# A hybrid mLSTM and RWKV-7 encoder layer: the mixer's TensorE steps taken in the written order

## The chip, the core and the metric

The kernel runs on one core of a Trainium2 chip. The metric is the device time of one execution in microseconds (us); it is the median of several executions. The core has a matrix engine (TensorE, PE in the rows), a vector engine (VectorE, DVE), an activation engine (ScalarE, ACT), GpSimd (POOL) and SyncE (SP, which issues most transfers). Each engine works through its own queue of instructions in order, and waits where an instruction needs a result that another engine has not yet delivered.

## What is computed

One encoder layer for 2048 tokens of width 1024. Only the mixer matters here, and the preparation of the attention behind it:

```python
h = rmsnorm(x, norm_mix);  p = h @ w_in
# first half of the columns: mLSTM, 4 heads of 128, chunks of 64
q, k = silu(causal_dwconv(p_qk));  gates = p_gates + m_gate_b
logf = log_sigmoid(f_pre);  b = cumsum(logf)            # per chunk
p    = exp(b_t - b_s + logi_s - m_t) * (q @ k.T)        # causal
h    = (s_int * (c_prev @ q) + p @ v) / max(|den|, exp(-m_t))
# second half: RWKV-7, 8 heads of 64, one state per head
sk    = state @ kk
state = state * w - outer(sk, kk * a) + outer(v, k);  y = state @ r
y_r   = (groupnorm(y) + sum(r * k * r_rk) * v) * sigmoid(gd) @ r_g_up
x = x + concat(y_m, y_r) @ w_out
kv = rmsnorm(mem) @ w_kv      # 256 memory rows, for the cross attention
```

Behind it come the cross attention to mem, a gated feed-forward network with a short convolution, and a last norm. All inputs and outputs are float32.

## The kernel before

**Tiling.** `mixer()` takes the tokens in 4 blocks of TB = 512. Each block needs 31 column groups of the projection (first x14, which holds the inputs of the gates, then x12 and the r, k, v and q, k, v, o groups), each as 24 dense matmuls of 128 by 512: the weights and the activations are split into a high and a low part, and three of the four products are computed for 8 slices of the depth. The rest of the mixer comes in units of one mLSTM head, or two RWKV heads, over one block; there are 16 units of each kind.

**Streams.** The work is written as generators, each of which yields after a small piece. `st_dense` (projection, `proj`, tile pd), `st_gates` (the gates of a block, `gates`, L486), `st_ml` (an mLSTM unit, `mlstm`, L833), `st_pre` (an RWKV unit's inputs and the small matrices of its chunks, last tile pab), `st_merge` (merges the solved matrices), `st_seq` (`rwkv_seq`, L730: the chain of 8 steps over the chunks of a unit) and `st_tail` (`rwkv_tail`, L774: group norm, transposes py, gate pg). `run_streams` (L1071) goes through them by a reckoned clock and writes next the first stream in the order s, g, a, t, m, p, d that is ready by that clock. A stream says with `yield` how long its next piece will have to wait for other engines; these waits are numbers of nanoseconds at L279 to L282, for instance LE and LME ahead of the mLSTM's pn and LSOLVE ahead of a merge. LG, the wait ahead of the gates' transposes, is 0:

```python
        LF, LG, LGD, LQK, LFD, LME, LM1 = 1590, 0, 1147, 3611, 844, 676, 3063
        ...
        order = dict(a=st_gates, s=st_seq, t=st_tail, m=st_ml, g=st_merge, p=st_pre, d=st_dense)
        run_streams([order[c]() for c in "sgatmpd"])
        kv_prep(kt, sm, T, PQ, PD)
```

**What sets the order.** The order in which the streams are written is not the order in the engines' queues. A scheduler takes the written instructions and puts those of each engine in an order of its own, by its own reckoning of what is ready when. That holds for all five engines and for the whole mixer.

**Names.** Nearly all matmuls of the mixer go through `mm` and `tr`, so their lines are L122 and L126; the tiles tell them apart. Gates: pd (of x14), then the chain L488 to L522 on ScalarE and VectorE over 4 rows, then four transposes gtr and their copy gc (L533). mLSTM unit: transposes pvt and pkt, products pst (k with q), e (L858 to L866, ScalarE and VectorE), then four times pn and pc, at the end the transposes pht. RWKV unit: pab; pt, p and pe belong to the solve and the merge. Each step of `rwkv_seq`: products into qy, ScalarE's copy q (L747), pu, VectorE's copy UV (L755), pS, VectorE's new state sbd (L761), further products into qy, ScalarE's copy yt.

**kv_prep** (L171) is called at the end of `mixer()`. For the norm of mem it needs two small matmuls mbc; then it handles 4 heads, each with eight weight loads of 512 KB (two of w_k, two of w_qT, two of w_v, two of w_ov) and the matmuls kps, qkps, kps again and vops, 672 in all. A weight load (`load_w`, L112) takes one of two raw buffers and is split by ScalarE (high) and GpSimd or VectorE (low).

Of the kernel before, what the change touches and what calls it, by code (L numbers as in the profile page):

```python
# [56 lines left out]
def tile_hybrid_encoder(ctx: ExitStack, tc: tile.TileContext, t_in: dict, out: bass.AP, stage: str = "all"):  # L57
# [1055 lines left out]
        kv_prep(kt, sm, T, PQ, PD)  # L1113
        mx.close()

    mixer()
    wld[0] = 0
    if stage == "mix":
        nc.sync.dma_start(out, y_dram.rearrange("k p t -> (k p) t"))
# [361 lines left out]
```

## Time and profile before

| | us |
|---|---|
| median of 3 runs | 3570.65 (3564.45 to 3571.49) |
| the profiled execution: its own time | 3564.44 |
| its span in the trace | 3562.6 |
| TensorE busy, of the span | 3377.6 (95%) |
| VectorE busy | 2020.6 (57%) |
| ScalarE busy | 1256.2 (35%) |
| GpSimd busy | 1368.7 (38%) |

The span is the time from the first to the last record of the profiled execution. The mixer takes the first 1431 us of it, the rest of kv_prep lasts until about 1514, and the attention and the feed-forward network the rest. Busy shares of the whole span hide that VectorE is far busier in the mixer than behind it; the table of stretches below has that. In the rows, a float32 matmul through L122 is recorded twice, so x8 in the trace is x4 in the order; transposes are recorded once, and so are the dense matmuls.

### The profile page before, as it was taken

What the parts mean: (1) busy time and instruction counts of PE and PEld (TensorE: products, weight loads), DVE (VectorE), ACT (ScalarE), POOL (GpSimd) and SP (SyncE); (2) the same over time, 40 slices, a digit from 0 to 9 for tenths busy, and PEclk for the clock granted to TensorE, in tenths of its full rate; (3) what the DMA queues carried; (4) which work ended last, traced back from release to release, by engine and by line L of the source; (5) the groups of instructions that cost most, each with busy time, mean ns of one, the idle gap of its engine ahead of it and who ended that gap; (6) DMA issues with size and microseconds to landing.
All of it is one profiled execution on the core that took longest, in us unless ns stands there. A gap on an engine that the chain in (4) does not pass through costs nothing.

```text
span 3562.6 us, 48272 instructions
## 1 busy us (share of the span) xinstructions
PE 3377.6 (95%) x17836; PEld 2750.2 (77%) x17836; DVE 2020.6 (57%) x4038; ACT 1256.2 (35%) x2397; POOL 1368.7 (38%) x1364
## 2 busy tenths in 40 slices
PE   7999999999989999789999999999999999999997
PEld 5777777777767778668888888888788888888886
DVE  6788888878888887433333343444453344344345
ACT  5345434544454444433222212212442222222213
POOL 5233333433333322353144434434632343443433
PEclk9999999999999999899999999999999999999998
DMA  4223222322222234685621111112566411111111
GB/s 131 80 67 111 77 72 75 111 70 68 90 73 69 73 94 146 212 269 177 222 71 43 59 42 54 54 36 71 154 219 212 141 55 36 54 54 42 54 48 54
DMA packets 203388, 342.01 MB, mean 96 GB/s; under 512 B 77072, under 2 KB 108944, under 8 KB 203152
## 3 DMA queue, kind: packets, MB, share of 16 engines
q1 hardware_dynamic: 203152, 338.92, 30.2%
q8 instruction: 141, 2.31, 0.3%
q14 instruction: 95, 0.78, 0.1%
HBM read 293.68 MB, written 45.15 MB: 95 GB/s over the span
## 4 chain that ended last, share of the span: by engine, by line
PE 55%; DMA 4%; DVE 2%; ACT 1%; issue 0%; POOL 0%; SPq 0%; DVEq 0%; ACTq 0%; POOLq 0%
PE pd L148 11%; PE pd L151 11%; PE pd L150 11%; PE dps L1354 4%; PE dps L1352 4%; PE dps L1353 4%; DMA x<-xT 2%; PE sc L1233 1%; PE sc L1235 1%; PE sc L1234 1%; DVE x L1369 0%; DMA wqk<-qk_dram 0%; PE ppt L1258 0%; DVE x L1201 0%; DMA y<-y_dram 0%
## 5 line engine op out<-in xcount | busy, mean ns | idle before, releaser
L105 POOL TENSOR_TENSOR wlo<-wraw,whi 128x512 fp32r<-128x512 f32 (+1 forms) x544 | 785.7, 1451 | 813.0 <-ACT whi L101 736.3
L122 PE MATMUL pd<-hA,whi 128*128 128x512 f32 x1984 | 677.6, 415 | 11.2 <-ACT uconv L824 5.8
L101 ACT CAST whi<-wraw 128x512 fp32r<-128x512 f32 (+1 forms) x596 | 383.4, 651 | 540.9 <-PE pd L150 222.0
L151 PE MATMUL pd<-h,wlo 128*128 128x512 f32 x1408 | 547.9, 389 | 0.0
L148 PE MATMUL pd<-h,whi 128*128 128x512 f32 x1408 | 547.9, 389 | 0.0
L150 PE MATMUL pd<-h,whi 128*128 128x512 f32 x1408 | 547.7, 389 | 0.0
L122 PEld LDWEIGHTS pd<-hA,whi 128*128 128x128 f32 x1984 | 357.5, 191 | 80.4 <-ACT hA L363 8.3
L122 PE MATMUL pd<-hA,wlo 128*128 128x512 f32 x992 | 402.2, 405 | 0.0
L1355 DVE TENSOR_TENSOR x<-dps,x 128x512 f32<-128x512 f32 x352 | 235.5, 689 | 224.3 <-PE dps L1354 222.2
L150 PEld LDWEIGHTS pd<-h,whi 128*128 128x128 f32 x1408 | 264.3, 188 | 54.8
L151 PEld LDWEIGHTS pd<-h,wlo 128*128 128x128 f32 x1408 | 264.3, 188 | 54.8
L148 PEld LDWEIGHTS pd<-h,whi 128*128 128x128 f32 x1408 | 264.3, 188 | 54.7
L1354 PE MATMUL dps<-act,wlo 128*128 128x512 f32 x704 | 271.5, 390 | 0.0
L1353 PE MATMUL dps<-act,whi 128*128 128x512 f32 x704 | 271.4, 390 | 0.0
L1352 PE MATMUL dps<-act,whi 128*128 128x512 f32 x704 | 261.6, 390 | 3.2 <-DVE x L1355 2.6
L122 PEld LDWEIGHTS pd<-hA,wlo 128*128 128x128 f32 x992 | 189.8, 191 | 34.2 <-issue 0.7
L1336 DVE SCALAR_TENSOR_TENSOR fu<-fu,pd 128x512 f32<-128x512 f32 x88 | 60.5, 688 | 226.6 <-PE pd L151 221.7
L1155 POOL TENSOR_TENSOR sq<-sq 128x512 f32<-128x512 f32 x56 | 73.9, 1320 | 252.9 <-ACT sq L1152 231.5
L1352 PEld LDWEIGHTS dps<-act,whi 128*128 128x128 f32 x704 | 132.6, 188 | 31.9 <-DVE x L1355 3.4
L1354 PEld LDWEIGHTS dps<-act,wlo 128*128 128x128 f32 x704 | 132.6, 188 | 27.6
L1353 PEld LDWEIGHTS dps<-act,whi 128*128 128x128 f32 x704 | 132.4, 188 | 27.5
L1330 POOL TENSOR_TENSOR fu<-fu,bcs 128x512 f32<-128x512 f32 x88 | 114.2, 1298 | 97.1 <-DVE fu L1329 95.6
(913 smaller groups left out, 6220.2 us busy)
## 6 DMA issues: line engine op xcount, KB each, us to landing
wraw<-w_in SPq DMA_DIRECT2D x124, 512.0 KB, 3.5
wraw<-f_up SPq DMA_DIRECT2D x88, 512.0 KB, 3.4
wqk<-qk_dram SPq DMA_DIRECT2D x64, 512.0 KB, 5.3
wvo<-vo_dram SPq DMA_DIRECT2D x64, 512.0 KB, 4.2
wraw<-f_down SPq DMA_DIRECT2D x44, 512.0 KB, 3.4
wraw<-w_out SPq DMA_DIRECT2D x32, 512.0 KB, 5.6
y<-y_dram SPq DMA_DIRECT2D x32, 256.0 KB, 7.0
x<-xT SPq DMA_DIRECT2D x32, 256.0 KB, 5.1
```

The costliest lines, as they stand in the source:

```text
L101: nc.scalar.copy(hi, raw)
L105: (nc.vector if dve else nc.gpsimd).tensor_tensor(lo, raw, hi.bitcast(F32), ALU.subtract)
L122: nc.tensor.matmul(out_, lhsT, rhs, **kw)
L148: nc.tensor.matmul(ps, hi[:, k % 4, :], a[:, 0, :n], start=(k == 0), stop=False)
L150: nc.tensor.matmul(ps, hi[:, k % 4, :], a[:, 1, :n], start=False, stop=False)
L151: nc.tensor.matmul(ps, lo[:, k % 4, :], a[:, 0, :n], start=False, stop=(k == last and not late))
L1155: (nc.vector if fast else nc.gpsimd).tensor_tensor(acc, acc, sq, ALU.add)
L1330: nc.gpsimd.tensor_tensor(u, u, bc3[b], ALU.mult)
L1352: nc.tensor.matmul(ps, hi[:, d, :], a[:, 0, :], start=(g == 0), stop=False)
L1353: nc.tensor.matmul(ps, hi[:, d, :], a[:, 1, :], start=False, stop=False)
L1354: nc.tensor.matmul(ps, lo[:, d, :], a[:, 0, :], start=False, stop=(g == GRP - 1))
L1355: nc.vector.tensor_tensor(xs[b][d], ps, xs[b][d], ALU.add)
```

## The change

`mixer()` is called inside a context that asks for a manual schedule of TensorE:

```diff
-    mixer()
+
+    with tc.manual_schedule(engines={mybir.EngineType.PE}):
+        mixer()
```

Within it TensorE's instructions stand in its queue exactly in the order in which the program writes them, that is, in the order that `run_streams` comes to, with all of kv_prep's matmuls behind that. VectorE, ScalarE, GpSimd and SyncE are still put in order by the scheduler. No instruction is added or taken away, and the blocks behind the mixer are untouched.

TensorE, the gates of block 1, before. The last matmul of x14 (tile pd_3275 there) stands 86 rows above gtr; what stands directly ahead of gtr is a later column group, pd_3812:

```order
L122 MATMUL pd_3812<-hA_3263,whi_3808 128x512 x2
L122 MATMUL pd_3812<-hA_3263,wlo_3810 128x512
L122 MATMUL pd_3812<-hA_3269,whi_3808 128x512 x2
L122 MATMUL pd_3812<-hA_3269,wlo_3810 128x512
L126 MATMUL gtr_3418<-ident_63,xs_3368 128x128 x4
L126 MATMUL pvt_3434<-ident_63,mv_3067 128x128 x4
L126 MATMUL pkt_3435<-ident_63,uconv_3058 128x128 x4
L122 MATMUL pS_3750<-UV_2426,E_2405 128x128
```

The same place now; pd_3277 is x14 of block 1:

```order
L122 MATMUL pd_3277<-hA_3259,whi_3194 128x512
L126 MATMUL pt32_3356<-ident_63,dg1_200 32x32 x8
L122 MATMUL pd_3277<-hA_3265,whi_3194 128x512
L122 MATMUL pd_3277<-hA_3271,whi_3194 128x512
L126 MATMUL gtr_3420<-ident_63,xs_3370 128x128 x4
L126 MATMUL pvt_3436<-ident_63,mv_3069 128x128 x4
L126 MATMUL pkt_3437<-ident_63,uconv_3060 128x128 x4
L122 MATMUL pst_3453<-uconv_2975,uconv_3060 128x128 x4
```

The transposes gtr have moved from 86 rows behind the end of x14 to the row directly behind it. In ScalarE's queue, 13 instructions of other steps stood between the first and the last step of this block's gate chain before, and 2 stand there now.

TensorE, mLSTM unit 14, from its transposes pvt to its first product pn, before:

```order
L126 MATMUL pvt<-ident,mv 128x128 x4
L126 MATMUL pv<-ident,xs 128x128
L126 MATMUL pkt<-ident,uconv 128x128 x4
L126 MATMUL pv<-ident,xs 128x128
L122 MATMUL pst<-uconv 128x128 x4
L122 MATMUL p_13460<-dg_199,tw 32x32 x8
L122 MATMUL pab<-KR,E 128x128 x3
L126 MATMUL pe<-ident,E 128x128 x2
L122 MATMUL pab<-KR,E 128x128 x5
L126 MATMUL py<-ident,yt 128x128 x4
L122 MATMUL pg<-sg_11153,gup_173 128x512
L122 MATMUL pg<-sg_10759,gup_175 128x512
```

The next row there is `L122 MATMUL pn<-v_13435,e 128x129`. The same unit now:

```order
L126 MATMUL pvt<-ident,mv 128x128 x4
L126 MATMUL pkt<-ident,uconv 128x128 x4
L122 MATMUL pst<-uconv 128x128 x4
L122 MATMUL p_13462<-dg_201,tw 32x32 x8
L126 MATMUL pe<-ident,E 128x128 x2
L122 MATMUL pn<-v_13437,e 128x129
L122 MATMUL pn<-cm_300,sib 128x129
```

The products pab, py and pg of other streams have left the place between pst and pn.

TensorE, the first two steps of the seq unit 14, before; mbc and kps are kv_prep's:

```order
L122 MATMUL qy<-UV,F 66x64 x2
L184 MATMUL mbc<-ident,mrs 128x128 x2
L122 MATMUL pu<-q,dg_197 66x64 x2
L122 MATMUL p_14565<-dg_198,tw 32x32 x8
L126 MATMUL pe<-ident,E 128x128 x4
L122 MATMUL pS<-UV,E 128x128
L122 MATMUL qy<-UV,F 128x64 x2
L148 MATMUL kps<-mem,whi 128x256 x2
L122 MATMUL qy<-sbd_1_289,KR 128x128
L122 MATMUL qy<-UV,F 66x64 x2
L150 MATMUL kps<-mem,whi 128x256
L151 MATMUL kps<-mem,wlo 128x256
```

TensorE, the end of the mixer now, the last seq step of unit 15 and what follows:

```order
L122 MATMUL pu<-q,dg_202 66x64 x2
L122 MATMUL pS<-UV,E 128x128
L122 MATMUL qy<-UV,F 128x64 x2
L126 MATMUL py<-ident,yt 128x128 x4
L122 MATMUL pg<-sg_11155,gup_175 128x512
L122 MATMUL pg<-sg_10761,gup_177 128x512
L184 MATMUL mbc<-ident,mrs 128x128 x2
L148 MATMUL kps<-mem,whi 128x256
L150 MATMUL kps<-mem,whi 128x256
L151 MATMUL kps<-mem,wlo 128x256
```

All of kv_prep's matmuls have moved from among the last two seq units to behind the last py and pg.

## Rows read from the trace of the kernel before

**Rows 1.** Stretches: us, busy us (count) by engine, PEclk, DMA share, GB/s.
```profile
107.00:1337.00 1230.00, 1142.36 (x7485) 898.91 (x7483) 1010.40 (x2511) 556.28 (x1174) 418.55 (x482) 0.98 0.27 81
684.00:688.00 4.00, 3.31 (x20) 2.89 (x21) 3.84 (x16) 2.37 (x6) 1.31 (x2) 0.50 0.41 63
1337.00:1431.00 94.00, 82.41 (x676) 72.91 (x674) 66.76 (x173) 43.41 (x107) 28.35 (x25) 0.93 0.48 147
1431.00:1525.00 94.00, 68.82 (x386) 59.07 (x385) 39.12 (x50) 38.02 (x70) 29.03 (x23) 0.84 0.72 223
```

**Rows 2.** Groups of TensorE, 0 to 1337 us: busy, mean ns | idle before, releasers.
```profile
L122 PE MATMUL pS<-UV,E 128*128 128x128 f32 x224 | 50.3, 307 | 41.8 <-DVE UV L755 39.4 <-DVE pm L479 1.9
...
L122 PE MATMUL pn<-v,e 128*128 128x129 f32 x128 | 27.4, 295 | 2.6 <-DVE e L866 2.6
...
L126 PE MATMUL gtr<-ident,xs 128*128 128x128 f32 x16 | 3.8, 382 | 15.0 <-ACT xs L515 15.0
```

**Rows 3.** Timeline of TensorE, x14's end and gtr: start, us, instruction, [idle before].
```profile
325.21 0.73 PE L122 MATMUL pd<-hA,whi 128*128 128x512 f32 x2
...
347.73 0.66 PE L126 MATMUL gtr<-ident,xs 128*128 128x128 f32 x4 [2.28 <-ACT xs L515]
...
658.45 0.74 PE L122 MATMUL pd<-hA,whi 128*128 128x512 f32 x2
...
684.70 1.12 PE L126 MATMUL gtr<-ident,xs 128*128 128x128 f32 x4 [2.56 <-ACT xs L515]
```

**Rows 4.** Timeline of ScalarE inside the gates of block 1.
```profile
333.11 0.61 ACT L101 CAST whi<-wraw 128x512 fp32r<-128x512 f32 x1
333.73 1.28 ACT L494 ACT_TABLE_LOAD   x1
```

**Rows 5.** Timeline of TensorE, mLSTM unit 1, then unit 14.
```profile
154.37 0.66 PE L126 MATMUL pvt<-ident,mv 128*128 128x128 f32 x4
...
163.27 0.39 PE L122 MATMUL pn<-v,e 128*128 128x129 f32 x2
...
1244.97 0.60 PE L126 MATMUL pvt<-ident,mv 128*128 128x128 f32 x4
...
1246.24 1.16 PE L122 MATMUL pst<-uconv 128*128 128x128 f32 x8
1247.33 0.69 PE L122 MATMUL p<-dg,tw 32*32 32x32 f32 x16
...
1248.59 0.44 PE L126 MATMUL pe<-ident,E 128*128 128x128 f32 x2
...
1251.41 0.39 PE L122 MATMUL pn<-v,e 128*128 128x129 f32 x2
```

**Rows 6.** Timeline of TensorE, the last pab, a seq step, the last py.
```profile
1334.24 0.93 PE L122 MATMUL pab<-KR,E 64*128 64x128 f32 x8
...
1418.48 0.47 PE L122 MATMUL qy<-sbd,KR 128*128 128x128 f32 x2
1418.78 0.40 PE L122 MATMUL qy<-UV,F 128*66 128x64 f32 x4
...
1419.59 0.45 PE L122 MATMUL pu<-q,dg 128*66 128x64 f32 x4
...
1420.42 0.49 PE L122 MATMUL pS<-UV,E 128*128 128x128 f32 x2
1420.74 0.56 PE L122 MATMUL qy<-UV,F 128*128 128x64 f32 x4
...
1430.44 0.89 PE L126 MATMUL py<-ident,yt 128*128 128x128 f32 x4 [3.44 <-DVE yt L788]
```

**Rows 7.** Timelines of SyncE's DMA issue (w_k, heads 2 and 3) and TensorE.
```profile
1431.06 0.34 SPq L96 DMA_DIRECT2D wraw<-w_k  x1
...
1469.55 0.33 SPq L96 DMA_DIRECT2D wraw<-w_k  x1
...
1513.23 0.39 PE L237 MATMUL vops<-whi,kvT 128*128 128x512 f32 x1
```

## The prediction, made before the result was known

> **What bounds the kernel now.** I first read the table of stretches [rows 1] to see which engine fills the part that the change touches. The mixer and the preparation of the attention's weights behind it run from the start to about 1525 us; nothing behind that is touched. From 107 to 1337 us, TensorE is busy for 1142 of 1230 us (93%) and VectorE for 1010 (82%); from 1337 to 1431 it is 82 of 94, and from 1431 to 1525 only 69 of 94. So TensorE sets the pace of the mixer, with VectorE not far behind it. A new order can save at most what TensorE now waits, and it costs whatever wait it opens, unless another engine had to wait longer anyway.
>
> Then I read the groups of TensorE up to 1337 us for the waits [rows 2]. The largest is 41.8 us ahead of pS, of which 39.4 wait for VectorE's copy of pu into UV (L755). The transposes gtr of the gates wait 15.0 us in all, the first product pn of the mLSTM units 2.6 us. These are small for the chains that stand behind them, and the timelines [rows 3, 5] show why: the scheduler has put other streams' matmuls between the two ends of each chain. What the change does to time is therefore what becomes of that cover. I went through the two orders of TensorE and looked, for each of these chains, at what stands between its ends before and now.
>
> **The change, part by part.** No instruction is added or taken away; the matmuls, their sizes and their data are the same. Only TensorE's order is another, and the other engines follow it. Four places matter.
>
> *First, the gates, four times.* The gate transposes gtr need the last column block x14 of the projection, and then a chain of ScalarE and VectorE steps on 4 rows. In block 1 x14 ends at 325.94 and gtr starts at 347.73, 21.8 us later; in block 2 it is 659.19 to 684.70, 25.5 us [rows 3]; the two other blocks give 24.6 both. Before, 83 to 88 rows of the order lie between them and TensorE waits only 2.3 and 2.6 us here at the end (15.0 in all four, [rows 2]). In the written order gtr stands directly behind x14's last matmul, because the planned latency ahead of gtr is LG = 0. So TensorE stands still for the whole chain. The chain itself may be shorter: in block 1 before, 13 instructions of other steps stand in ScalarE's queue inside it, now 2. At 0.61 us for such a one, as the weight cast [rows 4], 11 fewer give up to 6.7 us, and 21.8 becomes about 15. I take 20 us, a little more than the middle of 15 and 21.8, since VectorE's part of the chain has no such gain in the order. Cost: 4 × 20 = 80 less the 15 paid already, **+65**. Low end 4 × 15 − 15 = 45, high end 4 × 25.5 − 15 = 87.
>
> The chain holds two loads of ScalarE's function table, each 1.28 us [rows 4]. The Trainium skill, "ScalarE: Activation LUTs", section "What ACT_TABLE_LOAD costs", puts some 1.38 us of draining beside each load, 2.66 us for a switch. In the trace the cast ahead of the load ends where the load starts, so no such extra shows there; by the page's figure the floor of the four chains would rise by an estimated 4 × 2 × 1.38 = 11 us, and the sum with it.
>
> *Second, the mLSTM units, sixteen times.* Between the transposes pvt and the first product pn lie the exponentials e and their product with pst. In unit 14 before, pvt starts at 1244.97 and pn at 1251.41, 6.4 us; in unit 1 it is 154.37 to 163.27, 8.9 us [rows 5]. Before, TensorE fills this with products of other streams (pab, py, pg). In the written order 13 of the 16 units have only pvt, pkt, pst, one group of p and one of pe there. By the rows of unit 14 that is 1.27 (start of pvt to start of pst) + 1.09 (pst to p) + 0.69 + 0.44 = 3.5 us [rows 5], less an estimated 0.6 for two pv that stood in the first stretch and for the overlap of the last durations: 2.9. The three units behind a gate have 6.3 us or more there and are left out. If the chain keeps its 6.4 us, each unit waits 3.5 us: 13 × 3.5 = 45.5, less 2.6 paid before [rows 2], **+43**. High end with unit 1's chain: 13 × (8.9 − 2.9) − 2.6 = 75. Low end 23: half of it comes back, since during such a wait VectorE works off what pS now waits for [rows 2].
>
> *Third, the end of the mixer.* Before, the matmuls of the preparation (kps, qkps, vops) fill the last two seq units, which for lack of anything else would be a bare chain of small steps; 295 of its 672 matmuls are done at 1431. The last pab ends at 1335.17 and the last py starts at 1430.44 [rows 6]: 95 us in which the chain solve, merge, seq, tail of the last units runs. In the written order all of the preparation's matmuls stand behind the last pg, so this stretch holds the chain alone, and the preparation follows. Without the other work in its queues the chain gains a little; I take 5 us. The preparation's own pace stands in the loads of w_k: head 2's first at 1431.06, head 3's at 1469.55, 38.5 us a head [rows 7]. All four heads behind the chain: 4 × 38.5 = 154. Before, from py at 1430.44 to the last vops at 1513.62 [rows 7], it was 83. The difference is 71; the first weight buffers can be loaded and split while the chain runs, an estimated half a head (19 us), but the norm of mem, its split and the first kps (an estimated 14 us from their steps) come anew behind mbc, and 5 to 6 us of the last tail's evacuation no longer overlap. So 71 − 19 + 14 + 6 = 72, less 5 of the chain: **+67**. Low end 40 if the seq chain loses 20 us for emptier queues and the buffers give another 10; high end 93 if nothing is preloaded and the new start is paid.
>
> *Fourth, the seq steps.* Each of the 128 steps has two round trips, qy to q on ScalarE and pu to UV on VectorE. In both orders there are mostly three dense matmuls between pu and pS, so the wait for UV should stay near its 41.8 us [rows 2]. But before, these were chosen by the scheduler for the moment, and now they are fixed. I take **+5**; the bounds are 0 and +70.
>
> Sum: 65 + 43 + 67 + 5 = +180, on the profiled execution's 3564.4 us (span 3562.6): **3744 us**. The profiled one is the fastest of the three runs, 0.17% under the median of 3570.65; the sum by the median would be 3751, inside the error of the terms.
>
> **The rivals.**
>
> *Worse: VectorE's queue decides each seq step.* VectorE is 82% busy [rows 1], and with TensorE's order fixed, a VectorE queue that runs a microsecond late at pu delays pS and all that is queued behind it. Before, something else could be put ahead; now nothing. For: 39.4 of the 41.8 us ahead of pS wait for just this [rows 2]. Against: waits elsewhere let VectorE catch up. If each of the 112 steps before 1337 pays 0.7 us more, it is the bound of +70 instead of +5: 3744 + 65, about 3809, with longer gate chains up to 3830.
>
> *Milder.* ScalarE's queue is short in the gate chain (45), half of the pn waits come back (23), and the preparation is overlapped more by its loads (40): +108, and with 15 to 20 us of pS waits gone because VectorE caught up in them, about 3655.
>
> *Clock.* Behind block 2's wait for gtr the granted clock is 0.50 in the 4 us from 684, and from 1431 its mean is 0.84 against 0.98 in the mixer [rows 1]. In the bare chain at the end TensorE will be mostly idle; if it is granted half (1.2 of 2.4 GHz) there, the own matmuls of a step, 0.47 + 0.40 + 0.45 + 0.49 + 0.56 = 2.4 us [rows 6], may cost up to as much again, for 16 steps 38 us: 3782. The Trainium skill, "TensorE: Matmul & The Clock Gate", section "HAM oscillation — how this bites in real kernels", says that work which waits between bursts starts each burst at half clock again, and pays it every time. That supports this rival for the end and, less, for the pn waits; the trace's 0.84 behind 1431 agrees in direction, no row shows its size.
>
> *Faster.* The written order keeps the steps of the seq chain at an even distance, while before the scheduler's choices let pS wait 41.8 us and pn 2.6 [rows 2]. If these waits went, the gate chains fell under 4 us each (so nothing lost there) and the preparation were hidden by its loads, 44 us would be gained: about 3520. It decides only if gtr and the last py find their inputs ready, and the chains of 21.8 and 95 us [rows 3, 6] speak against it strongly.
>
> *No change.* The edit could do nothing if TensorE's order were already the written one. The orders differ at all four places, so this is nearly out.
>
> **How the numbers follow.** My forecast (3700 to 3800) has 0.58, worse (3800 to 3860) 0.17, milder (3620 to 3700) 0.14, the clock 0.05, faster 0.04, no change 0.02. The likeliest is 3744. The range: below it I leave out faster, no change and half of milder (0.13), above it some of the worse (0.05): 3660 to 3840. The ends of the four terms all at once (+108 and +325) would be 3672 and 3889; all high together I do not expect, since a longer wait in one place shortens the others. Faster by over 0.2% (about what a measurement of this kernel can tell from no change): 0.04; within 0.2%: 0.02; slower: 0.94.
>
> **What would show it right or wrong.** After the change: four gaps of 15 to 22 us on TensorE ahead of gtr, released by ScalarE's L515, with a sum of 60 to 87 us; a wait of 3 to 5 us ahead of the first pn of 13 units, released by VectorE's L866, about 50 us in all; no kps, qkps or vops ahead of the last pg, and 140 to 160 us from the last py to the last vops; a wait ahead of pS of 40 to 60 us in sum. The part behind the preparation should take as long as before. The forecast is wrong if the waits ahead of gtr are short (the chain then had slack that I did not see), if the waits ahead of pS grow past 100 us (VectorE's queue decides), or if the seq steps at the end run much faster than 95 us for the chain, so that the preparation starts early.

## The result, and the profile after

The changed kernel takes 3930.18 us (median of 4, 3926.39 to 3935.35) against 3567.55 before: 1.1017 times as long, 95% interval 1.0997 to 1.1037. That is 363 us more, twice the forecast of 180. The direction was right; the size was far outside the range. One of the four executions of before_no_solve, a version further down, took 7597 us; that version's time is given as the median of the other three.

The table of stretches of the changed kernel, cut at the last pab, the last py and the last vops (us, busy us (count) of PE, PEld, DVE, ACT, POOL, then PEclk, DMA share, GB/s):

```profile
0.00:1622.50 1622.50, 1319.55 (x7834) 1044.33 (x7835) 1051.81 (x2651) 623.99 (x1283) 473.95 (x587) 0.88 0.23 69
1622.50:1729.00 106.50, 71.57 (x397) 58.16 (x395) 42.75 (x136) 18.70 (x57) 6.84 (x5) 0.53 0.05 14
1729.00:1879.50 150.50, 120.45 (x683) 104.12 (x681) 64.23 (x86) 60.87 (x117) 48.37 (x40) 0.85 0.64 203
```

The same cuts before lie at 1335.2, 1430.4 and 1513.6; the first stretch there is

```profile
0.00:1335.20 1335.20, 1220.90 (x7831) 961.34 (x7832) 1077.36 (x2649) 615.82 (x1284) 474.11 (x588) 0.98 0.28 84
```

So the mixer up to the last pab is 287 us longer, the chain at the end 11, the preparation behind it 67, and what follows 1. The mixer is where the forecast failed: the forecast had 113 us for it. Two things are to be seen in its row. TensorE is idle for 303 us (1622.5 less 1319.55), where it was 114 before; and its busy time for the same matmuls rose by 99 us, with a granted clock of 0.88 against 0.98. 189 and 99 make the 287.

The waits, from the groups of TensorE up to the last pab after the change (busy, mean ns of one | idle before, releasers):

```profile
L122 PE MATMUL pS<-UV,E 128*128 128x128 f32 x224 | 53.2, 322 | 95.1 <-DVE UV L755 94.0
L122 PE MATMUL qy<-sbd,KR 128*128 128x128 f32 x224 | 52.6, 320 | 33.4 <-DVE sbd L761 32.0 <-ACT yt L768 0.8
L122 PE MATMUL pn<-v,e 128*128 128x129 f32 x126 | 38.8, 402 | 29.0 <-DVE e L866 27.2 <-ACT tw L706 1.8
L122 PE MATMUL pc<-v,kw 128*128 128x129 f32 x126 | 33.0, 354 | 4.3 <-DVE E L724 4.2
L126 PE MATMUL pe<-ident,E 128*128 128x128 f32 x116 | 27.5, 325 | 10.2 <-DVE dg L716 7.5 <-DVE cm L884 2.7
L126 PE MATMUL gtr<-ident,xs 128*128 128x128 f32 x16 | 4.5, 434 | 73.0 <-ACT xs L515 73.0
```

Against [rows 2]: gtr 15.0 to 73.0 (+58), pn 2.6 to 29.0 (+26), pS 41.8 to 95.1 (+53); qy went from 12.5 to 33.4 (+21), with this line before:

```profile
L122 PE MATMUL qy<-sbd,KR 128*128 128x128 f32 x224 | 47.3, 293 | 12.5 <-DVE sbd L761 11.9 <-ACT yt L768 0.3
```

The four make 159 of the 189; the rest is spread over pe, pab, pd, p, pc and others. The gates look as forecast, here block 1's on TensorE's timeline, to be set beside [rows 3]:

```profile
384.58 0.73 PE L122 MATMUL pd<-hA,whi 128*128 128x512 f32 x2
403.57 1.11 PE L126 MATMUL gtr<-ident,xs 128*128 128x128 f32 x4 [18.25 <-ACT xs L515]
```

**The late seq steps.** The 53 us ahead of pS are not a little more at each of the 112 steps. From the trace I took, for each step, the time from pu's end to the start of VectorE's copy UV. 20 steps are over 2 us late, 92 us in sum. Before the change it was 19 steps, 96 us in sum: VectorE was just as late. What differs most is what TensorE has to do in the meantime: before, 68 us of matmuls stood in these 19 steps, now 12.5 in the 20. What VectorE does in these steps differs as well. After the change a piece of the solve of the small RWKV matrices (L656 and L658, or L676 and L678) stands ahead of UV in all 20; before it was 12 of the 19, and in the other seven VectorE worked mostly for the gates, the mLSTM or an RWKV unit's inputs. One such step before, first VectorE's timeline, then TensorE's:

```profile
871.27 1.58 DVE L676 TENSOR_TENSOR pr<-n,l 128x256 f32<-128x256 f32 x3
...
878.46 0.68 DVE L678 TENSOR_REDUCE x<-pr 128x32 f32<-128x512 f32 x1
879.05 0.28 DVE L755 COPY UV<-pu 64x128 f32<-64x128 f32 x1
```

```profile
870.67 0.40 PE L122 MATMUL pu<-q,dg 128*66 128x64 f32 x4
870.87 0.70 PE L122 MATMUL pd<-hA,whi 128*128 128x512 f32 x2
...
878.60 0.73 PE L122 MATMUL pd<-hA,whi 128*128 128x512 f32 x2 [0.92 <-DVE xs L482]
...
879.40 0.47 PE L122 MATMUL pS<-UV,E 128*128 128x128 f32 x2
```

And one after the change, in the same order:

```profile
552.01 2.55 DVE L676 TENSOR_TENSOR pr<-n,l 128x256 f32<-128x256 f32 x3 [1.14 <-DMA d<-rd]
...
558.22 0.56 DVE L676 TENSOR_TENSOR pr<-d,x 128x256 f32<-128x256 f32 x1
558.71 0.27 DVE L755 COPY UV<-pu 64x128 f32<-64x128 f32 x1
```

```profile
552.11 0.40 PE L122 MATMUL pu<-q,dg 128*66 128x64 f32 x4
552.32 0.72 PE L122 MATMUL pd<-hA,whi 128*128 128x512 f32 x2
552.88 0.40 PE L122 MATMUL pd<-hA,wlo 128*128 128x512 f32 x1
559.03 0.79 PE L122 MATMUL pS<-UV,E 128*128 128x128 f32 x2 [5.75 <-DVE UV L755]
```

In both, VectorE runs the second half of the solve (L676 and L678, some 7 us in one piece) ahead of UV. Before, products of other streams, most of them the projection's, fill TensorE from 870.87 to 879.4 with 0.92 us of waiting; now three of them stand there, and TensorE waits 5.75 us.

**The clock.** By the granted clock of the first row, (1 − 0.88) / 0.5 × 1622.5 = about 390 us of the mixer are at half clock. The trace has 48 such stretches there, 398 us in sum; before it was 13 with 61 us. Of the 48, 45 begin in or right behind a wait of TensorE: 4 in gtr's waits, 30 behind one of 2 to 6 us, 11 behind one of 1 to 2 us. One, behind a short wait for pn (timeline, then the table of stretches):

```profile
278.59 0.77 PE L122 MATMUL pn<-v,e 128*128 128x129 f32 x2 [2.30 <-DVE e L866]
```

```profile
278.10:298.50 20.40, 18.36 (x94) 15.17 (x95) 7.90 (x34) 2.93 (x8) 0.00 (x0) 0.50 0.04 4
```

The wait is 2.3 us, and the 20 us behind it run at 1.2 GHz, the lower of the clock's two levels, with TensorE busy for 18.4 us. The Trainium skill, "TensorE: Matmul & The Clock Gate", section "HAM oscillation — how this bites in real kernels", says that bursts with waits between them start at half clock each time; this trace agrees in those 45 stretches.

**The end.** The preparation behind the last py, on TensorE and on SyncE's queue, beside [rows 7]:

```profile
1728.59 1.09 PE L126 MATMUL py<-ident,yt 128*128 128x128 f32 x4 [6.26 <-DVE yt L788]
...
1733.51 0.39 PE L148 MATMUL kps<-mem,whi 128*128 128x256 f32 x1 [1.01 <-ACT mem L161]
```

```profile
1760.08 0.33 SPq L96 DMA_DIRECT2D wraw<-w_k  x1
...
1798.44 0.33 SPq L96 DMA_DIRECT2D wraw<-w_k  x1
```

The heads follow each other by 38.4 us, as before, and all four lie behind the last py now.

### The profile page after: what moved, and what is told of

It is laid out like the page before. It is cut to its first block, busy times and chain, and to the rows that moved or that the text cites. A ratio compares the mean times of both kernels' runs of the same rounds, so it can differ in the third digit from the quotient of the medians.

```text
span 3929.8 us, 48318 instructions
## 1 busy us (share of the span) xinstructions
PE 3520.8 (90%) x17836; PEld 2865.0 (73%) x17836; DVE 1996.1 (51%) x4038; ACT 1265.5 (32%) x2397; POOL 1369.1 (35%) x1364
## 4 chain that ended last, share of the span: by engine, by line
PE 71%; DVE 13%; DMA 5%; ACT 4%; issue 3%; POOL 2%; SPq 1%; DVEq 0%; ACTq 0%; POOLq 0%
PE pd L148 11%; PE pd L151 11%; PE pd L122 11%; PE pd L150 11%; PE dps L1356 4%; PE dps L1355 4%; PE dps L1354 4%; PE qy L122 2%; DVE pr L656 2%; DVE pr L676 2%; PE pab L122 1%; PE sc L1235 1%; PE sc L1237 1%; PE sc L1236 1%; PE pn L122 1%
## 5 line engine op out<-in xcount | busy, mean ns | idle before, releaser
L122 PE MATMUL pd<-hA,whi 128*128 128x512 f32 x1984 | 692.4, 430 | 16.6 <-ACT hA L363 6.6
L122 PEld LDWEIGHTS pd<-hA,whi 128*128 128x128 f32 x1984 | 360.1, 200 | 87.0 <-ACT hA L363 16.1
L122 PE MATMUL pd<-hA,wlo 128*128 128x512 f32 x992 | 404.2, 407 | 0.0
L122 PEld LDWEIGHTS pd<-hA,wlo 128*128 128x128 f32 x992 | 196.8, 198 | 44.6
L122 PE MATMUL pS<-UV,E 128*128 128x128 f32 x256 | 65.6, 343 | 104.8 <-DVE UV L755 103.8
```

Source lines behind the costliest of these rows:

```text
L122: nc.tensor.matmul(out_, lhsT, rhs, **kw)
```

## The experiments

Each is the changed kernel with an edit, unless it says otherwise. Theory A: other engines' chains are as long as before, and what is lost is their cover, the matmuls that stood inside them. Theory B: a rigid order makes VectorE's queue later, so that cover only moves a wait. Theory C: the half clock behind each wait is a cost of its own. The executions of one version lie 2 to 22 us apart, so a difference of some 10 us between two medians says little.

**kv_free.**

```diff
-        run_streams([order[c]() for c in "sgatmpd"])
+        with tc.manual_schedule(engines={mybir.EngineType.PE}):
+            run_streams([order[c]() for c in "sgatmpd"])
...
-    with tc.manual_schedule(engines={mybir.EngineType.PE}):
-        mixer()
+    mixer()
```

> TensorE's written order holds only for the streams; the preparation of keys and values (kv_prep) is scheduled freely again. Theory A (what is lost is the cover: matmuls that stood inside other engines' chains): the stretch from the last pab to the last vops, 257 us after the change and 178 before, returns to 175 to 195, and the part ahead of the last pab stays at 1622 us: 3930 - 70 = 3860 (3845 to 3875). Theory B (the seq chain at the end is itself lengthened by the rigid order): the preparation's matmuls amid its steps lengthen it, the gain stays under 40: above 3890.

Measured: 3853.2 us, 77 less than the change. Its table of stretches with the same cuts:

```profile
1627.90:1733.00 105.10, 92.86 (x723) 80.02 (x722) 70.23 (x178) 47.53 (x114) 31.65 (x28) 0.91 0.46 140
1733.00:1809.00 76.00, 62.01 (x357) 53.35 (x355) 35.20 (x44) 32.21 (x60) 23.32 (x18) 0.89 0.73 230
```

The end chain is as long with the matmuls amid it (105.1 against 106.5), and the preparation behind it falls from 150.5 to 76.0. Inside the chain two things cancel: with the clock at 0.91 instead of 0.53 the steps of the last seq unit follow each other by some 3.4 us instead of 4.6, but its first step comes later. The third term is right, and it is apart from the rest.

**gates_cover.** `LG` 0 becomes 20000.

> LG, the planned wait ahead of the gates' transposes gtr, is 20000 instead of 0, so that 80 and more rows of other streams stand between x14 and gtr again. Theory A: the wait ahead of gtr falls from 73.0 us to 5 to 15; with the half clock behind these waits (21 us of work in it) the time falls by 58 to 70: 3860 to 3875. Theory B (while TensorE waits there, VectorE works off what the other waits would have been for): half of it comes back ahead of pS and pn, gain 20 to 35: 3895 to 3910.

Measured: 3887.0, a gain of 43, between the two. TensorE's groups:

```profile
L122 PE MATMUL qy<-sbd,KR 128*128 128x128 f32 x224 | 54.7, 331 | 49.1 <-DVE sbd L761 46.7 <-ACT yt L768 2.4
...
L126 PE MATMUL gtr<-ident,xs 128*128 128x128 f32 x16 | 2.6, 283 | 2.0 <-ACT xs L515 2.0
```

The 71 us ahead of gtr are gone, but 16 of them are back ahead of qy, and some at other places. This fits theory B of this expectation, that VectorE had caught up while TensorE stood at gtr; no run shows it by itself.

**pn_cover.** `LME` 676 becomes 4500.

> LME, the planned wait ahead of the mLSTM's first pn, is 4500 instead of 676, so that 4 us more of other matmuls stand ahead of pn. The waits ahead of pn are 29.0 us in sum after the change, but 114 us of TensorE's work lies in half-clock stretches that begin behind one of them. Theory A with the clock (each wait is paid a second time by the half clock behind it): -29 + some 3 that stay, and up to 57 more: 3850 to 3880. Theory A without the clock: only the waits go, 3900 to 3910.

Measured: 3897.0, a gain of 33. The profiled execution is the fastest of the four, at 3886.2. In it the waits ahead of pn fell from 29.0 to 4.2, the waits of the mixer by 18 in all, its busy time by 28 (1319.6 to 1291.4): more came from the clock than from the waits, but not the 57 that I had allowed, since pe and others wait where pn did (pe 10.2 to 17.6).

**fill_pn**, which tests the clock alone: useless work in place of the waits.

```diff
+                if c == 0:
+                    t_ = pe[0]
+                    for _ in range(FILN.get(un[0], 0)):
+                        mm(pn[:, 0, 0:128], k2[:, 0:P], q2[:, 0:P], start=True, stop=True)
+                    pe[0] = t_
+                    un[0] += 1
```

FILN, above the part shown, holds the number of products for each unit.

> The changed kernel with 83 useless float32 products (128 by 128, about 0.27 us each, 22 us in all) put ahead of the first pn of the ten mLSTM units that waited there (26 us in all); their result is overwritten. Nothing else of the order changes. Theory C (the half clock that follows a wait is a cost of its own): the stretches at half clock behind pn, 130 us with 114 us of TensorE's work in them, go, and the time falls by 40 to 57 although TensorE has more to do: 3873 to 3890. Rival (the clock falls for another reason, or what it costs is hidden by VectorE anyway): the same or longer, 3925 to 3945.

Measured: 3901.5, a gain of 29. The mixer's stretch and TensorE's groups of pn (the second group is the filler):

```profile
0.00:1598.50 1598.50, 1308.44 (x8000) 1039.28 (x8001) 1053.23 (x2651) 623.43 (x1283) 471.89 (x587) 0.90 0.23 70
```

```profile
L122 PE MATMUL pn<-v,e 128*128 128x129 f32 x126 | 31.3, 335 | 4.8 <-DVE e L869 2.9 <-ACT tw L706 1.8
L122 PE MATMUL pn<-uconv 128*128 128x128 f32 x166 | 27.8, 337 | 8.0 <-DVE E L724 6.1 <-ACT tw L711 1.9
```

TensorE has 28 us more to do (22 at full clock) and is busy 11 us less in all, and the mixer's waits fell by 13 (303 to 290). The orders of the other engines are the same but for a swapped pair in each. So the products that were there before take 33 to 39 us less, and little but the clock has changed for them: theory C stands, with a smaller gain than it forecast (3873 to 3890).

**fill_uv**, the same at the seq steps: `mm(qyb[:, 256:384], KR[:, c, :], sb, start=True, stop=True)` n times behind pu, into the rest of qy's bank. The values that come out differ with these fillers; the order and the count of TensorE's other work don't.

> The changed kernel with 307 useless float32 products (about 83 us in all) between pu and pS in the 22 seq steps that waited over 1.5 us there (89 us in all), sized by each wait, into an unused part of qy's bank. Theory C: the half clock behind these waits (about 102 us with 89 us of work in it) goes, up to -44; where VectorE's order comes out a little different a filler misses its wait and adds to the time instead: 3890 to 3920. Rival: nothing comes back, 3930 to 3960.

Measured: 3943.8, 14 more. The wait ahead of pS fell from 95 to 30, that ahead of qy rose from 33 to 63, and TensorE's busy time rose by 56. The fillers themselves took about 74 us by the trace (the expectation had 83), so the other products take some 18 us less, which fits the clock; much of the wait was paid again at the next step. As a test of the clock's price it is inconclusive: VectorE's order changed with it, and 14 us is little beside the spread of the executions.

**uv_cover.** `LU` 178 becomes 5000, and py waits for a closed step.

> LU, the planned wait between pu and pS in every seq step, is 5000 instead of 178, so that some 5 us of other matmuls stand between them (the tail's py waits until a seq step is closed, since both use one PSUM buffer). After the change 20 steps find VectorE's copy UV over 2 us late, as 19 did before; only the cover is gone. Theory A: the wait ahead of pS falls from 95 us (up to the last pab) to under 30, the half clock behind it goes (89 us of work in it, 44 us lost): 3930 - 70 - 40 = 3820 (3800 to 3850). Theory B (VectorE's queue is made late by the rigid order): the lateness moves along with it, the waits stay above 60, 3890 or more.

Measured: 3953.6, 23 more; theory A's forecast failed here. TensorE's groups up to its last pab:

```profile
L122 PE MATMUL qy<-sbd,KR 128*128 128x128 f32 x224 | 60.4, 359 | 100.7 <-DVE sbd L764 84.8 <-ACT yt L771 15.0 <-ACT sw L546 0.8
...
L122 PE MATMUL pS<-UV,E 128*128 128x128 f32 x224 | 48.5, 301 | 3.0 <-DVE UV L758 3.0
...
L122 PE MATMUL pg<-sg,gup 128*128 128x512 f32 (+1 forms) x39 | 28.8, 1101 | 49.1 <-DVE sbd L764 49.1
```

The wait left pS (95 to 3) and is back ahead of qy, and ahead of pg, which shares one PSUM buffer with pu and pS. The order of the program shows why. VectorE is still ordered by the scheduler, which puts the solve where TensorE's order leaves room. In the order of the changed kernel 21 pieces of the solve of some 3 us or more stand ahead of a UV and none ahead of an sbd; in uv_cover it is 1 and 26.

**late_steps_cover.** Cover on both sides, only where VectorE's order has a piece of the solve. The lists LATE_UV and LATE_SB, not shown, name the steps and the length of their waits.

```diff
-                yield LU
+                yield LATE_UV.get(sk[0], LU)
...
-                yield LS
+                yield LATE_SB.get(sk[0] - 1, LS)
```

> The changed kernel with cover only where VectorE's order has a piece of the solve ahead of UV or ahead of the new state sbd: 24 seq steps get a planned wait of 3 to 6 us (as long as the piece) between pu and pS, 18 get 2 to 6 us behind the step; py waits for a closed step as in uv_cover, and pg for the end of such a wait. Theory A (same lateness as before the change, lost cover): with the cover put back on both sides the waits ahead of pS and qy fall from 128 us to under 60, with the clock behind them 70 to 118 us come back (118 is what leaving the solve out gained here beyond what it gained before): 3812 to 3860. Rival (a fixed order can't follow VectorE; as in uv_cover the wait moves on): above 3900.

Measured: 3912.4, a gain of 18: the rival's number. TensorE's groups:

```profile
L122 PE MATMUL qy<-sbd,KR 128*128 128x128 f32 x224 | 50.8, 310 | 50.8 <-DVE sbd L768 38.2 <-ACT yt L775 6.4 <-ACT ya L823 5.0
L122 PE MATMUL pS<-UV,E 128*128 128x128 f32 x224 | 47.8, 295 | 25.1 <-DVE UV L762 24.8
L122 PE MATMUL pu<-q,dg 128*66 128x64 f32 x448 | 47.3, 231 | 24.2 <-DVE ya L831 18.3 <-DVE pm L479 5.8
...
L126 PE MATMUL py<-ident,yt 128*128 128x128 f32 x52 | 9.3, 306 | 11.7 <-ACT yt L775 11.7
```

pS and qy together fell from 128 to 76, but pu now waits for ya, the consumer of pg, which came between two steps and holds their buffer, and py for its own. The mixer's waits are 301 us in sum, as with the change alone. So a cover by planned waits doesn't bring the time back; whether the solve is the cause had to be shown in another way.

**no_solve and before_no_solve** take the suspected cause away, in the changed kernel and in the kernel before; without the solve the values that come out are other ones:

```diff
-            for i in range(14, -1, -1):
+            for i in range(0):
...
-            for rhs in (n12, d22):
+            for rhs in ():
```

> The changed kernel without VectorE's loops in rwkv_solve (the products and sums of the forward substitution are left out, its transfers stay), so that VectorE's queue has no burst in front of UV. To be read against the kernel before with the same loops left out. Theory A (the burst was as late before, and covered then): here it gains much, the wait ahead of pS falls from 95 us to under 35, with the clock behind it 100 to 150 us, and the chain at the end is 25 us shorter too: 3760 to 3810. Rival (the rigid order itself, not VectorE's lateness, makes the waits): under 60 in the mixer, above 3850.

> The kernel before without VectorE's loops in rwkv_solve. Theory A: since the burst is covered there by matmuls that the scheduler put between pu and pS (68 us in 19 late steps), leaving it out gains only the 40 us that TensorE waited in these steps and some of the chain at the end: 3500 to 3550. Rival: as much as with the changed order, 3420 to 3470.

Measured: 3775.6, 154.5 less than the change, and 3525.5, 39 less than before (3564.6 in the same comparison). The other expectations go by 3528 and 36 for the latter, and so by 118 for the difference. Both came as theory A has it, though not each reading behind it: of the 41.8 us ahead of pS before, the 19 late steps hold 23, not 40. TensorE's groups, first of no_solve, then of before_no_solve:

```profile
L122 PE MATMUL qy<-sbd,KR 128*128 128x128 f32 x224 | 48.5, 299 | 20.4 <-DVE sbd L761 17.7 <-ACT yt L768 1.1
...
L122 PE MATMUL pS<-UV,E 128*128 128x128 f32 x224 | 46.8, 291 | 8.1 <-DVE UV L755 6.7 <-DVE pm L479 0.5
```

```profile
L122 PE MATMUL pS<-UV,E 128*128 128x128 f32 x224 | 46.7, 291 | 14.0 <-DVE UV L755 11.8 <-DVE pm L479 1.9
L122 PE MATMUL qy<-sbd,KR 128*128 128x128 f32 x224 | 46.1, 287 | 6.8 <-DVE sbd L761 5.8 <-ACT yt L768 0.6
```

The same VectorE work costs 154.5 us under the written order and 39 under the scheduler's. The difference, about 115 us, is what the written order loses at the solve, with the clock behind it. That it is the solve's pieces, and not VectorE's load in general, rests on the trace of the changed kernel, where a piece of the solve stands ahead of UV in all 20 late steps; no run left out another part of VectorE's work. The chain at the end, which I had expected 25 us shorter, stayed at 105.6.

**three_covers**, **all_covers** and **three_covers_no_solve** put the edits together.

> kv_free, gates_cover and pn_cover in one: the preparation scheduled freely, LG 20000, LME 4500. If the three costs are apart from each other their gains add, 77 + 43 + 33: 3777 (3760 to 3800). If they share VectorE's lateness or the clock: 3800 to 3840.

> three_covers with cover at the late seq steps as in late_steps_cover (lists made anew for this order: 24 steps ahead of pS, 17 ahead of the next qy). Theory A: 3777 less 70 to 118, 3660 to 3710; what then stays over the time before is the small waits at pe, p, pc, pab and pd. If lateness just moves on: above 3740.

> three_covers without VectorE's loops in rwkv_solve (as in no_solve). three_covers stands at 3756, the kernel before without the loops at 3528. Theory A (what three_covers still loses is mostly VectorE's solve, for which the written order has no matmuls at the right places): the waits ahead of pS and qy, 136 us in three_covers, fall under 40, and the time by 120 to 160: 3595 to 3635, so that the remaining cost of the order over the kernel before, 185 us with the solve, is about 90 without it. Rival (the rest is spread over all small chains, whatever VectorE does): it falls by the 36 us that the kernel before gained, to above 3690.

Measured: 3755.6, 3733.8 and 3611.3. The first three gains add, and a little more: 175 against 153, so that the time lies just under the range. The cover at the late steps brings another 22 only, between the two theories. Leaving out the solve brings 144 in three_covers (39 in the kernel before). What is then still over before_no_solve is 86 us (102 between the two profiled executions). By the traces it lies in the mixer, with 65 us more of waits and 52 us more of busy time; what follows the mixer is 16 us shorter. TensorE's groups of three_covers_no_solve up to its last pab show where the waits are:

```profile
L122 PE MATMUL pd<-hA,whi 128*128 128x512 f32 x1984 | 679.9, 424 | 15.3 <-ACT hA L363 8.4 <-DVE xs L482 2.6 <-DVE pm L479 2.3
L122 PE MATMUL pab<-KR,E 64*128 64x128 f32 x512 | 63.3, 360 | 17.3 <-ACT UV L622 12.1 <-DVE bv L598 4.4
...
L122 PE MATMUL pc<-v,kw 128*128 128x129 f32 x126 | 31.4, 338 | 13.3 <-DVE den L889 5.3 <-DVE E L724 5.2 <-ACT tw L711 1.4
L126 PE MATMUL pe<-ident,E 128*128 128x128 f32 x116 | 26.1, 310 | 27.0 <-DVE dg L716 15.2 <-DVE E L724 5.6 <-DVE og L911 3.1
```

These four wait 73 us here and under 6 in before_no_solve. No version that keeps the solve comes near the kernel before: the nearest, all_covers, has 3733.8 against 3570.3.

## Why the prediction was wrong

*Gates.* Forecast +65, measured +58 in waits. The chain was 18.2 us in all four blocks, within the 15 to 21.8 read from [rows 3, 4]; right. As a part of the time it is worth 43 (gates_cover), most likely because VectorE catches up during these waits.

*mLSTM.* Forecast +43, measured +26 in waits, near the low end of 23; with the clock behind them the term is 33 (pn_cover). The sign and place were right. Counting all 13 units at the full chain of 6.4 us was too much: ten units waited, by 1.9 to 4.3 us each.

*End.* Forecast +67, measured +79: the preparation +67, where I had +72, and the chain +11, where I took −5. The chain ran at a clock of 0.53, as the clock rival said, and its last steps took 4.6 us where they took some 3.4 before; the rival's price of 38 us was too high. The term as a whole is right in size, and confirmed by kv_free (77).

*Seq steps.* Here the working failed. The step "in both orders there are mostly three dense matmuls between pu and pS, so the wait for UV should stay near its 41.8 us" went by what is usual, when the wait comes from the unusual. [Rows 2] give only the sum; the trace of the kernel before, read step by step, had the rest: in 12 of the steps 2.6 to 7.5 us of matmuls stand between pu and pS, seven of them against a piece of VectorE's solve. I took +5; the waits ahead of pS and qy rose by 74, and the solve costs about 115 more under the new order (no_solve against before_no_solve). The rival "VectorE's queue decides each seq step" was nearer: it said that nothing else could be put ahead of a late pS any more, and it had the size of the waits (+70). But it spread them over each step, by 0.7 us (for 112 steps that is 78, not 70). In sum VectorE is no later than before, the loss is in 20 steps, each with a piece of the solve, and the rival had no clock behind them.

*Clock.* I had priced it for the bare chain at the end only (+38). It is the second missed term: TensorE's busy time up to the last pab rose by 99 us for the same matmuls. The rows had it, as 0.50 behind one wait for gtr [rows 1], but the sum priced every new wait at its own length. fill_pn shows that the clock is a cost apart: with 28 us of useless products in place of waits, the kernel is 29 us faster.

*Small waits.* pe, pab, pd, p, pc and pt were not costed at all; together about 30 us of waits, and most of the waits that three_covers_no_solve still has over before_no_solve are there.

*The range.* "A longer wait in one place shortens the others" is true to a degree (gates_cover, uv_cover), but it was used to hold down the upper end, while the clock makes each wait dearer. Gates, mLSTM and end were forecast at 175, and three_covers gives back 175; that the sums agree is in part luck, since the forecast priced waits alone and the gain has the clock in it. Of the 363 us, by these runs, 175 belong to the three, 105 to the solve (144 less 39), and 86 are left for the small chains (366 in sum, within the spread of the executions); the clock is in all of them.

What stays open: how the 99 us of the clock divide between the waits, since fill_uv was disturbed; what the small chains cost each, since no run covers them; and why a cover at just the late steps gives so little. The shared buffers and the moving solve explain where the waits went, but no fixed order that covers both sides was found by planned waits alone.

## What to carry to other kernels

Before an order is replaced, look at how a wait is spread over its instances: a sum that comes from few late ones is covered by an order made for these, and the usual step tells nothing. Price a new wait on TensorE with the slower clock behind it, not only with its own length. A cover on one side of a chain can move another engine's long piece of work to the other side, when that engine is still scheduled freely (uv_cover).

## What the runs showed of the hardware

In the changed kernel's mixer the granted clock stood at 0.50 in 48 stretches, and 45 of them began in or right behind a wait of TensorE, most often one of 2 to 6 us. TensorE's busy time for the same matmuls rose with it from 1220.9 to 1319.6 us. Replacing about 26 us of such waits by products that nobody needs made the kernel 29 us faster (3930.2 to 3901.5).
